# Two transformer blocks on one core: the SBUF pools in another order, and two buffer sizes changed, so that float32r operands start at multiples of 128 bytes

## Chip, cores and metric

One core of one Trainium2 chip. The metric is the device time of one execution in microseconds (us); lower is better.

## The reference, cut to what matters

Two blocks work on one sequence of 256 tokens with 2048 features, in float32. Block 1 mixes by attention (8 heads of 128) and by a gated linear recurrence, then runs 32 experts of which each token uses two, then a gated per-layer input. Block 2 has 16 self-attention heads of three kinds, an attention to 256 memory rows and a convolutional gated feed-forward of width 5632, and a last norm. Nearly all of the arithmetic is in the dense products with the weights:

```python
proj = hn @ w_in[i]                                       # 2048 x 5128, and a second one in block 2
h = h + jnp.concatenate([att_out, rnn_out], axis=-1) @ w_out[i]
hid = jax.nn.silu(t @ w_gate[e]) * (t @ w_up[e])          # experts
gate = jax.nn.sigmoid(rms_norm(h, ple_norm[i]) @ w_ple_gate[i])
# block 2, feed-forward: 2048 -> 2 x 5632 -> 2048
```

## The kernel before

**Products of high accuracy from float32r.** Every dense product is made three times. A weight arrives as float32 in a `raw` buffer. ScalarE copies 1024 columns of it, rounded to float32r, into a `hi` buffer (`split_hi`), and VectorE writes what the rounding lost into a `lo` buffer (`split_lo`). The tokens are kept in the same way as a pair of operands (`xth` and `xtl`, `xtuh` and `xtul`, and so on), in the big slots S0 to S5. A product is hi*hi + lo*hi + hi*lo, all in float32r, accumulated in PSUM; `mm` (line 506) issues each of these TensorE products.

There are two forms. In `form_a` a block of 128 weight columns is stationary, and all 256 tokens move: one product has 256 columns. In `form_b` the tokens, 128 at a time, are stationary and the weights move: one product has 512 columns. For each product the stationary operand is loaded anew (LDWEIGHTS, "PEld" in the profile).

**Order of the work.** The weights come as a list of units (`units`), at most 128 x 2048 float32, each loaded by the SyncE queue into one of 5 `raw` buffers. A unit is cut into quarters of 1024 columns. Each quarter takes the next of 4 `hi` and 4 `lo` buffers in turn, so quarter after quarter goes round the four buffers. In the up projection of the last feed-forward a quarter makes 2 x 4 x 3 = 24 products of 256 columns, in the down projection 2 x 2 x 3 = 12 products of 512 columns. All other work beside the products is written as tasks; a model of the engines' clocks (`clk`) decides at build time in which order instructions are emitted. Its costs are computed from the shapes of the operands that an instruction reads and writes, and not from the sizes or the addresses of the buffers that hold them. The experts (lines 1263 to 1565) work in float32 on the weights as they are loaded, and use the slots, the `raw` buffers and the `hi` and `lo` buffers as targets of their loads; the gathering and adding up of tokens around them is in float32r.

**Where the buffers lie.** A pool takes its place in each partition of SBUF in the order in which the pools are opened (lines 35 to 41), and within a pool the buffers lie one behind the other, each rounded up to 32 bytes. The pools begin at byte 16,512 of a partition, which is 129 x 128. First comes `per` with 25,632 bytes of constants and small tiles. So `slots`, 6 buffers of 16,384 bytes, begins at 42,144; that is 32 bytes past a multiple of 64, and 160 past a multiple of 256, and so does each slot in it. `stm` follows with 5 `raw` buffers of 4 x 520 x 4 = 8,320 bytes, then 4 `hi` and 4 `lo` buffers of 1040 x 4 = 4,160 bytes; 4,160 is 65 x 64. So the four `hi` buffers start at 32, 96, 160 and 224 bytes past a multiple of 256, and the four `lo` buffers likewise, in the same order. `wk`, 6 buffers of 2,048 bytes, and `sm` come last.

The operand slices add multiples of 512 bytes (`form_a`: 128 columns; `form_b`: 128 tokens of a row of 1024 bytes) or 1024 bytes to these starts, so a product's operands stand past a multiple of 256 as their buffers do. The one exception is the first product of block 1, whose units are 520 columns wide: there the blocks of 128 columns begin 8 columns (32 bytes) into a row, and the second row of a unit stands another 2,080 bytes on, so that some stationary operands start at multiples of 64 while the moving ones stay at 160 past a multiple of 256.

Of the kernel before, what the change touches and what calls it, by code (L numbers as in the profile page):

```python
# [30 lines left out]
def block_kernel(ctx: ExitStack, tc: tile.TileContext, A, out, stop=None, dbg=None, force_general=False):  # L31
# [3 lines left out]
    per = ctx.enter_context(tc.tile_pool(name="per", bufs=1))  # L35
    slots = ctx.enter_context(tc.tile_pool(name="slots", bufs=1))
    stm = ctx.enter_context(tc.tile_pool(name="stm", bufs=3))
    wk = ctx.enter_context(tc.tile_pool(name="wk", bufs=1))
    sm = ctx.enter_context(tc.tile_pool(name="sm", bufs=8))
# [7 lines left out]
    # ------------------------------------------------------------------ order of emission  # L47
    # Every engine takes its instructions in the order in which they are emitted. Work beside the matrix products
    # is cut into tasks: generators that name the engine ("a", "d", "p") before each of their steps. A model of
    # the engines' clocks (us) picks the step that can start first, so that no engine waits for another one  # L50
    # inside a chain while it has other work.
# [18 lines left out]
    class Vec:  # L70
        def __getattr__(self, name):
            f = getattr(nc.vector, name)

            def g(o, *a, **k):
                f(o, *a, **k)  # L75
                ins = [x for x in a[:3] if not isinstance(x, (float, int)) and x is not None]
                fast = name in ("tensor_scalar", "tensor_copy", "memset") and all(x.space != PSM for x in ins)
                t = 0.068 + o.free_size() * (0.00052 if fast else 0.00104)
                if name == "tensor_reduce":
                    t = 0.068 + ins[0].free_size() * 0.00104  # L80
                if name in ("tensor_scalar", "scalar_tensor_tensor") and not isinstance(a[1], (float, int)):
                    t += 0.06
                now = clk["d"]
                # an operand that the last instruction has just written costs its latency
                w = last.get("o")
                if o.free_size() <= 64 and any(x.tensor is w for x in ins):
                    t += 0.13
                last["o"] = o.tensor
                clk["d"] = now + t
            return g  # L90
# [4 lines left out]
    def mul(o, l, r, start, stop):  # L95
        """a product beside the stream"""
        nc.tensor.matmul(o, l, r, start=start, stop=stop, skip_group_check=True)  # L97
        clk["p"] += r.free_size() * (1 if r.dtype == F32R or r.dtype == BF else 4) / 2400.0 + 0.01
# [64 lines left out]
    def advance(t):  # L163
        """run the task to its next request; False when it has ended"""
# [17 lines left out]
    def settle(t):  # L182
        """resolve conditions and delays; True when the task asks for an engine"""
# [39 lines left out]
    def candidates(qs):  # L223
        """[(start, priority, run it, engine)]"""
# [16 lines left out]
    def pump():  # L241
        """what fits beside the products that have been emitted"""
# [32 lines left out]
    # ------------------------------------------------------------------ weight stream  # L275
# [86 lines left out]
    def raw_tile():  # L362
        return stm.tile([128, 4 * 520], F32, name="raw", tag="raw", bufs=RAWS)

    def hl_tiles(dtype):
        return (stm.tile([128, 1040], dtype, name="hi", tag="hi", bufs=HLS),
                stm.tile([128, 1040], dtype, name="lo", tag="lo", bufs=HLS))

    # buffers of the experts' weights: two slots in halves, the raw tiles, the tiles of the split weights, and
    # at first a third slot  # L370
# [13 lines left out]
    def exp_bufs(x):  # L384
# [3 lines left out]
        if k == "R":  # L388
            t = raw_tile()[:, 0:2048]
# [31 lines left out]
    # the third slot is free after the raw tiles and most of the split weights' that come behind it  # L421
# [12 lines left out]
    def split_steps_open():  # L434
        """the steps of splitting that could be next: [(start, quarter, run it)]"""
# [35 lines left out]
    def next_quarter():  # L471
# [11 lines left out]
        if EXP0 - RAWS <= u < EXP0:  # L483
            # the first of the experts' weights, as tiles get free
# [12 lines left out]
    def need_of(done):  # L497
        """products wait until the blocks up to kb are there"""
# [9 lines left out]
    def form_a(X, kbs, blocks, first, last, need=None, beside=True):  # L508
        """W stationary: blocks = [(psum out [128, S], column, first in its bank)]"""
# [21 lines left out]
    def form_b(X, kbs, banks, first, last, width=512, need=None):  # L531
        """X stationary: banks[tt] psum [128, <=512]"""
# [37 lines left out]
    # ------------------------------------------------------------------ start: loads and constants  # L570
# [13 lines left out]
    # x and the first weights in turns; when they are there, about  # L584
# [16 lines left out]
    def warm(n):  # L601
        """products that nobody reads: the tensor engine's clock rises only after some us of work"""
# [16 lines left out]
    # the other constants, as rows to be transposed  # L619
# [30 lines left out]
    def const_gen():  # L650
# [19 lines left out]
        # half biases of the gates; 2 softplus(-lam), by atanh's series for log1p  # L670
# [37 lines left out]
    # ------------------------------------------------------------------ norms: sums over d, 1/rms per token  # L708
    def rsqrt(n, ssq, scale):
        """[128, n] 1/sqrt(ssq * scale + EPS)"""  # L710
# [18 lines left out]
    def have_r():  # L729
        """the condition that the norm asked for last is there"""  # L730
# [3 lines left out]
    def spread(r):  # L734
        """[128 tok, 2] per-token factors -> [128, 256] on all partitions, in PSUM"""
# [5 lines left out]
    def set_r(ssq, wide):  # L741
        """a task's steps: R["r"] [128 tok, 2] and R["b"] [128, 256] from sums of squares [128 tok, 2]"""
# [32 lines left out]
    def add_sq(sq, t):  # L775
        """the sum of the blocks' squares, by one more"""
# [6 lines left out]
    def operand(dst, kb, gain, sq, t, done):  # L783
        """a task's steps: block kb of h times the gain as an operand, and its squares"""
# [10 lines left out]
    def resid_gen(o, kb, dst, gain, sq, done):  # L795
        """h += o; operand of the next norm"""
# [4 lines left out]
    def split_steps(dst, kb, src, done=None):  # L801
        """a task's steps: an operand of src"""
# [19 lines left out]
    # ================================================================== block 1: mixing  # L822
# [49 lines left out]
    def bias_rows_gen():  # L872
        """relative-position bias of block 2, to DRAM:
        bias_d[head, q, c] = row[head, 127 - q + c], queries 128..255 at keys 0..255"""
# [31 lines left out]
    # minus the sums of log f, in three parts that add up to it exactly, at partitions 0, 32 and 64  # L906
# [61 lines left out]
    def rnn_gen():  # L968
        """scan; rc becomes the state.
        a = exp(-y), s = tanh(y/2): 1/(1+s) = (1+a)/2, refined; a = 2/(1+s) - 1; sqrt(1-a^2) = 2 sqrt(s)/(1+s)"""  # L970
# [27 lines left out]
    # F and RX  # L998
# [17 lines left out]
    # Q, K: per-head norms, transposed  # L1016
# [48 lines left out]
    # attention of block 1  # L1065
    def max_of(srcs, biases, p, m):
        """scores + bias -> p [128, 384], -max in m[2:4]"""
# [13 lines left out]
    def pt_steps(p):  # L1081
        """P [128 q, 384] -> P^T: [128 s0, 256 t] | [128 s1, 128 t]"""
# [11 lines left out]
    def pv_t(t, v, dst, kb, done=None):  # L1094
        """out^T [dh, tok] = V^T P^T, split into dst"""
# [46 lines left out]
    # RG: gelu(rg) * state  # L1142
# [27 lines left out]
    # w_out; tokens in rows for the experts; scores of the router  # L1170
# [33 lines left out]
    def xn_gen(n, tt):  # L1204
# [9 lines left out]
        if n == 3:  # L1214
            # beside the routing on the vector engine
# [46 lines left out]
    # ================================================================== block 1: experts  # L1262
# [22 lines left out]
    # groups of a token: [128, (tt), 4]; experts: [128, (tt, group), 8]. The choice does not depend on the token's  # L1285
    # 1/rms, a positive factor of all its scores; the first of equal ones is taken
# [31 lines left out]
    # place among the expert's tokens from 1 on where selected, 0 elsewhere  # L1318
# [17 lines left out]
    def gather(q):  # L1336
        """the tokens of four experts' slots: xe, by steps of two of its 16 rows"""
# [22 lines left out]
    def weights():  # L1360
        """weights of the two experts, times 1/rms of the token; what goes past the slots"""
# [39 lines left out]
    def loadable(u):  # L1401
        """whether the unit's buffer has been read"""
# [14 lines left out]
    def hidden(i):  # L1417
        """the experts' hidden values of pair i, times the slots' weights, and room for their transpose"""
# [42 lines left out]
    def transposes(i):  # L1461
        """of the hidden values, and of G"""
# [29 lines left out]
    # the first pair's hidden values beside its gather  # L1492
# [13 lines left out]
    for i in range(16):  # L1506
# [7 lines left out]
        if i == 15:  # L1514
            # p^T as an operand
# [9 lines left out]
        for j in range(2):  # L1525
# [16 lines left out]
            if i == 15:  # L1542
                # the next weights are split in time for the products that follow
# [27 lines left out]
    # general path: the tokens past an expert's slots, by dense products over all tokens  # L1571
# [54 lines left out]
    # ================================================================== block 1: gated per-layer input  # L1626
# [52 lines left out]
    # ================================================================== block 2: self attention  # L1679
# [134 lines left out]
    # w_out_2; the memory's operands beside it  # L1814
# [81 lines left out]
    # ================================================================== block 2: memory attention  # L1896
# [98 lines left out]
    # ================================================================== block 2: conv-GLU  # L1995
# [25 lines left out]
    def tok_gen():  # L2021
        """h in place to tokens in rows: h[p, kb, (tt, c)]"""
# [64 lines left out]
    # w_down: hid split as it is used; tokens in rows  # L2087
# [22 lines left out]
    def fin_gen(bank, n, tt):  # L2110
        """h += products (tokens in rows), sums of squares; times the final gain, but for the last columns"""
# [37 lines left out]
    def last_columns(X, banks):  # L2149
        """the last products of the last two column blocks, one token tile after the other"""  # L2150
# [40 lines left out]
def _constants():  # L2191
    """rows of a product with [bias table; ones; dilated heads]: distance d = 255 - i of column i"""
# [42 lines left out]
```

## Time and profile before

| | |
|---|---|
| time, median of 3 runs | 2263.07 us (2262.58 to 2263.34) |
| span of the profiled execution, first to last instruction | 2260.5 us |
| the median less that span | 2.6 us |
| TensorE products in the trace | 15,552 |
| weights and inputs read from HBM | 510.61 MB |

PE is the matrix products, PEld the loads of stationary operands, DVE VectorE, ACT ScalarE. The products are pipelined: a row of the trace gives a product's whole passage through the array, and the next product starts well before it ends. What a product costs in a stream is therefore the distance from its start to the next start, called the pitch here. It is read from two starts and the number of products between them, or from a piece of the chain that has only such products.

### The profile page before, as it was taken

How to read it: one execution, taken by the hardware profiler on the slowest of the kernel's cores; microseconds unless marked ns; L12 is line 12 of the kernel's file. 1: busy time of each engine (PE TensorE's matmuls, PEld its weight loads, DVE VectorE, ACT ScalarE, POOL GpSimd, SP SyncE). 2: the span in 40 equal slices, each digit the busy share in tenths (PEclk: the TensorE clock that was granted, in tenths of full speed). 3: DMA queues.
4: the chain of work that ended last, by engine and by line, in shares of the span. 5: the costliest groups of instructions: out<-in, count | busy, mean ns of one | idle time of the engine just before them, and what ended most of it. 6: DMA issues, size and time to landing. Idle time of an engine off the chain costs nothing.

```text
span 2260.5 us, 37736 instructions
## 1 busy us (share of the span) xinstructions
PE 2210.5 (98%) x15552; PEld 1887.0 (83%) x15552; DVE 1264.3 (56%) x2251; ACT 943.7 (42%) x1493; POOL 34.0 (2%) x62
## 2 busy tenths in 40 slices
PE   9999979999999999999999999999999999999998
PEld 8888978555455565998999999999999999988886
DVE  8866654233333334875477558675655665564545
ACT  6745533211111112654444446455444444444443
POOL 1000000000000000000000000000000000000000
PEclk9999989999999999999999999999999999999999
DMA  8554668999999997465545556555555565555552
GB/s 282 168 180 164 144 189 304 332 403 396 401 398 396 399 394 276 171 196 194 185 153 170 181 180 192 184 169 170 187 187 188 185 195 191 191 200 193 186 187 93
DMA packets 232415, 517.30 MB, mean 229 GB/s; under 512 B 11783, under 2 KB 51446, under 8 KB 232112
## 3 DMA queue, kind: packets, MB, share of 16 engines
q1 hardware_dynamic: 229168, 506.57, 63.7%
q0 software_dynamic: 3040, 8.27, 1.8%
q8 instruction: 124, 2.03, 0.4%
q14 instruction: 51, 0.42, 0.1%
q10 hardware_dynamic: 32, 0.01, 0.0%
HBM read 510.61 MB, written 4.19 MB: 228 GB/s over the span
## 4 chain that ended last, share of the span: by engine, by line
PE 59%; DVE 0%; ACT 0%; ACTq 0%; issue 0%
PE acc L506 51%; PE sd L506 6%; PE sd L97 2%; PE sd L699 1%; DVE rs L75 0%; DVE hid L75 0%; DVE lo L75 0%; ACT hi L61 0%; ACT junk L61 0%; ACT out L61 0%; DVE h L75 0%; ACT cx L61 0%; DVE hs L75 0%; ACTq L2231 0%; ACT xtph L61 0%
## 5 line engine op out<-in xcount | busy, mean ns | idle before, releaser
L75 DVE TENSOR_TENSOR lo<-raw,hi 128x1024 fp32r<-128x1024 f32 (+1 forms) x572 | 698.6, 1224 | 549.2 <-ACT hi L61 544.1
L61 ACT ACTIVATE hi<-raw 128x1024 fp32r<-128x1024 f32 (+1 forms) x572 | 605.6, 1059 | 768.8 <-PE acc L506 649.2
L506 PE MATMUL acc<-xtuh,hi 128*128 128x256 f32 x1408 | 393.9, 280 | 0.0
L506 PE MATMUL acc<-xtul,hi 128*128 128x256 f32 x1408 | 393.6, 280 | 0.0
L506 PE MATMUL acc<-xtuh,lo 128*128 128x256 f32 x1408 | 393.2, 279 | 0.0
L506 PEld LDWEIGHTS acc<-xtuh,lo 128*128 128x128 f32 x1408 | 266.1, 189 | 0.0
L506 PEld LDWEIGHTS acc<-xtuh,hi 128*128 128x128 f32 x1408 | 266.0, 189 | 0.0
L506 PEld LDWEIGHTS acc<-xtul,hi 128*128 128x128 f32 x1408 | 265.8, 189 | 0.0
L75 DVE TENSOR_TENSOR h<-acc,h 128x512 f32<-128x512 f32 (+1 forms) x180 | 101.7, 613 | 196.0 <-PE acc L506 196.0
L506 PE MATMUL acc<-xt2h,hi 128*128 128x256 f32 x512 | 147.5, 288 | 0.0
L506 PE MATMUL acc<-xt2l,hi 128*128 128x256 f32 x512 | 143.4, 280 | 0.0
L506 PE MATMUL acc<-xt2h,lo 128*128 128x256 f32 x512 | 143.4, 280 | 0.0
L506 PE MATMUL acc<-hi,hs 128*128 128x512 f32 x352 | 112.0, 393 | 0.8 <-ACT hs L61 0.7
L506 PE MATMUL sd<-hi,hs 128*128 128x512 f32 x352 | 111.7, 393 | 0.0
L61 ACT ACTIVATE sg<-acc,ws 128x256 f32<-128x256 f32 x16 | 7.6, 475 | 243.6 <-PE acc L1445 148.2
L506 PEld LDWEIGHTS acc<-xt2h,hi 128*128 128x128 f32 x512 | 96.8, 189 | 4.1 <-issue 4.0
L506 PEld LDWEIGHTS acc<-xt2l,hi 128*128 128x128 f32 x512 | 96.9, 189 | 0.1
L506 PEld LDWEIGHTS acc<-xt2h,lo 128*128 128x128 f32 x512 | 96.7, 189 | 0.0
L75 DVE TENSOR_TENSOR yy<-acc,yy 128x512 fp32r<-128x512 f32 x64 | 44.3, 692 | 92.4 <-ACT yy L61 92.4
L506 PEld LDWEIGHTS acc<-gt,yy 128*128 128x128 f32 x512 | 64.4, 188 | 30.4 <-issue 27.7
L506 PE MATMUL acc<-oth,lo 128*128 128x256 f32 x256 | 72.8, 284 | 12.3 <-DVE lo L75 12.3
L506 PEld LDWEIGHTS acc<-hi,hs 128*128 128x128 f32 x352 | 66.0, 188 | 16.4 <-ACT hs L61 0.9
(390 smaller groups left out, 4711.3 us busy)
## 6 DMA issues: line engine op xcount, KB each, us to landing
raw<-in_w_up_dram SPq DMA_DIRECT2D x88, 1024.0 KB, 5.0
raw<-in_w_in_dram SPq DMA_DIRECT2D x52, 1024.0 KB, 5.2
raw<-in_w_down_dram SPq DMA_DIRECT2D x44, 1024.0 KB, 5.0
raw<-in_w_out_dram SPq DMA_DIRECT2D x32, 1024.0 KB, 5.1
raw<-in_w_in_dram SPq DMA_DIRECT2D x64, 512.0 KB, 4.5
raw<-in_w_expert_down_dram SPq DMA_DIRECT2D x29, 1024.0 KB, 10.1
raw<-in_w_expert_gate_dram SPq DMA_DIRECT2D x45, 512.0 KB, 10.0
raw<-in_w_expert_up_dram SPq DMA_DIRECT2D x45, 512.0 KB, 10.2
```

What stands on the lines that cost most here:

```text
L61: nc.scalar.activation(o, i, f, **k)
L75: f(o, *a, **k)
L97: nc.tensor.matmul(o, l, r, start=start, stop=stop, skip_group_check=True)
L506: nc.tensor.matmul(o, l, r, start=first, stop=last, skip_group_check=True)
L699: nc.tensor.transpose(o, i, idt)
```

## The change

The pool `per` is opened after `wk` and no longer first. The `raw` buffers become 2,048 elements (8,192 bytes) in place of 2,080, and the `hi` and `lo` buffers 1,056 elements (4,224 bytes, 33 x 128) in place of 1,040. The rest of the diff takes out comments and docstrings. No instruction is added, taken out or given another shape.

```diff
-    per = ctx.enter_context(tc.tile_pool(name="per", bufs=1))
     slots = ctx.enter_context(tc.tile_pool(name="slots", bufs=1))
     stm = ctx.enter_context(tc.tile_pool(name="stm", bufs=3))
     wk = ctx.enter_context(tc.tile_pool(name="wk", bufs=1))
+    per = ctx.enter_context(tc.tile_pool(name="per", bufs=1))
     sm = ctx.enter_context(tc.tile_pool(name="sm", bufs=8))
...
     def raw_tile():
-        return stm.tile([128, 4 * 520], F32, name="raw", tag="raw", bufs=RAWS)
+        return stm.tile([128, 2048], F32, name="raw", tag="raw", bufs=RAWS)
 
     def hl_tiles(dtype):
-        return (stm.tile([128, 1040], dtype, name="hi", tag="hi", bufs=HLS),
-                stm.tile([128, 1040], dtype, name="lo", tag="lo", bufs=HLS))
+        return (stm.tile([128, 1056], dtype, name="hi", tag="hi", bufs=HLS),
+                stm.tile([128, 1056], dtype, name="lo", tag="lo", bufs=HLS))
...
         if k == "R":
-            t = raw_tile()[:, 0:2048]
+            t = raw_tile()
```

By the same count as above `slots` now begins at 16,512, the `raw` buffers at 114,816, the `hi` buffers at 155,776, the `lo` buffers at 172,672 and `wk` at 189,568: all multiples of 128. Past a multiple of 256 the slots stand at 128, and the four `hi` and the four `lo` buffers at 128, 0, 128 and 0.

## Rows read from the trace of the kernel before

**Rows 1.** The page, its first part: span, and busy time by engine.

```profile
span 2260.5 us, 37736 instructions
PE 2210.5 (98%) x15552; PEld 1887.0 (83%) x15552; DVE 1264.3 (56%) x2251; ACT 943.7 (42%) x1493; POOL 34.0 (2%) x62
```

**Rows 2.** Busy time in stretches, line 506 alone: PE, PEld, granted clock, DMA share, GB/s.

```profile
11.00:200.00 189.00, 173.95 (x940) 146.72 (x939) 1.00 0.59 197
200.00:460.00 260.00, 157.03 (x1226) 150.40 (x1224) 0.96 0.74 239
...
905.00:1127.00 222.00, 219.34 (x1560) 205.51 (x1560) 0.99 0.57 188
1127.00:1326.00 199.00, 174.54 (x1392) 166.66 (x1392) 1.00 0.52 168
1326.00:1420.00 94.00, 91.01 (x767) 89.98 (x768) 1.00 0.56 180
1420.00:1558.00 138.00, 127.73 (x966) 120.24 (x966) 1.00 0.53 177
1558.00:2006.00 448.00, 447.28 (x3841) 447.08 (x3839) 1.00 0.58 188
2006.00:2260.50 254.50, 244.41 (x1056) 198.02 (x1056) 0.98 0.50 170
```

**Rows 3.** The same view, all instructions: PE, PEld, DVE, ACT, POOL busy, clock, DMA, GB/s.

```profile
0.00:57.00 57.00, 54.57 (x421) 50.49 (x421) 46.26 (x115) 35.27 (x62) 8.63 (x21) 1.00 0.82 280
452.00:509.00 57.00, 55.21 (x373) 32.94 (x370) 19.84 (x37) 9.87 (x21) 0.00 (x0) 1.00 1.03 403
...
791.00:848.00 57.00, 55.22 (x390) 34.42 (x388) 17.77 (x34) 8.23 (x19) 0.00 (x0) 1.00 1.02 394
```

**Rows 4.** The chain that ended last: start us, length us, what.

```profile
1557.90 444.46 PE acc L506 x3815
...
2023.15 11.09 PE acc L506 x48
```

**Rows 5.** Timeline of PE in the up projection, first products of five quarters in a row.

```profile
1700.45 0.28 PE L506 MATMUL acc<-xtuh,hi 128*128 128x256 f32 x1
...
1703.17 0.28 PE L506 MATMUL acc<-xtuh,hi 128*128 128x256 f32 x1
...
1706.01 0.28 PE L506 MATMUL acc<-xtuh,hi 128*128 128x256 f32 x1
...
1708.75 0.28 PE L506 MATMUL acc<-xtuh,hi 128*128 128x256 f32 x1
...
1711.63 0.28 PE L506 MATMUL acc<-xtuh,hi 128*128 128x256 f32 x1
```

**Rows 6.** The same view in the down projection: products of 512 columns.

```profile
2080.03 0.39 PE L506 MATMUL sd<-lo,hs 128*128 128x512 f32 x1
...
2080.71 0.39 PE L506 MATMUL sd<-lo,hs 128*128 128x512 f32 x1
...
2081.40 0.39 PE L506 MATMUL sd<-lo,hs 128*128 128x512 f32 x1
...
2082.10 0.39 PE L506 MATMUL sd<-lo,hs 128*128 128x512 f32 x1
```

**Rows 7.** The same view: plain float32 transposes, and float32 products in two passes.

```profile
55.33 1.89 PE L97 MATMUL sd<-vrc,qkT 128*128 128x256 f32 x8
...
1462.30 1.47 PE L699 MATMUL sd<-ident,pm 128*128 128x128 f32 x12
```

**Rows 8.** Lines, shapes kept apart: the splitting of the weights on DVE and ACT.

```profile
L75 DVE TENSOR_TENSOR lo<-raw,hi 128x1024 fp32r<-128x1024 f32 x564 | 688.7, 1224 | 546.3 <-ACT hi L61 541.2 <-PE sd L97 2.6 <-DMA eraw<-in_w_expert_up_dram 1.6
L61 ACT ACTIVATE hi<-raw 128x1024 fp32r<-128x1024 f32 x564 | 596.9, 1059 | 762.4 <-PE acc L506 648.4 <-PE sd L506 75.4 <-issue 24.8
```

**Rows 9.** The first product (units 520 columns wide), stationary at other offsets.

```profile
26.23 0.28 PE L506 MATMUL acc<-xth,hi 128*128 128x256 f32 x1
...
27.55 0.28 PE L506 MATMUL acc<-xth,lo 128*128 128x256 f32 x1
```

**Rows 10.** DMA issues on the page: KB each, us to landing.

```profile
raw<-in_w_up_dram SPq DMA_DIRECT2D x88, 1024.0 KB, 5.0
```

## Prediction

> **What bounds the kernel now.** I read the page's first part for who is busy, then the stretches for where, then the chain and the timeline for what one product costs. TensorE is busy for 2210.5 of 2260.5 us, VectorE for 56% and ScalarE for 42% [rows 1]. A busy PE alone does not say that PE is the bound, so the stages are read one by one. The line that issues the float32r products is busy for nearly the whole of every stretch after 905 us [rows 2]. One stage has another limit: in the experts, 460 to 905 us, the DMA engines are saturated up to about 850 us (share 1.02 and more, 394 to 403 GB/s) [rows 3], and a faster product there only waits longer for its weights. Between 200 and 460 us line 506 is busy for 157.03 of 260 us, with waits in between [rows 2].
>
> In the chain, 3815 products of 256 columns take 444.46 us with nothing between them, 116.5 ns each; 48 products of 512 columns take 11.09 us, 231 ns each [rows 4]. The granted clock is 1.00 in these stretches (2.4 GHz). One column a cycle would be 106.7 and 213.3 ns, so the stream loses 8% of both. The loss has a pattern. Quarter after quarter, with the same instructions and the same moving operands, the pitch changes: 2.72 us for 24 products is 113.3 ns, then 2.84 gives 118.3, 2.74 gives 114.2, 2.88 gives 120.0, and the cycle begins again [rows 5]. What differs is the weights' buffer, which stands at 96, 32, 224 and 160 past a multiple of 256. So addresses matter here, and in steps: 113.3 is 17 times 6.67 ns and 120.0 is 18 times, where 6.67 ns is 16 columns, 64 bytes of one partition. With 512 columns, three products take 0.68 us in one quarter and 0.70 in the next [rows 6]: 226.7 and 233.3 ns, 34 and 35 such steps. An operand of 1024 bytes that starts 32 past a multiple of 64 touches 17 pieces of 64 bytes; one that starts on a multiple touches 16. That is my reading. One thing is against it: 2048 bytes touch 33 pieces and not 34, so a long operand seems to pay twice.
>
> Two more rows bound what is left when the cost is gone. Twelve float32 transposes, each with its own load of 128 stationary columns, come at (1.47 - 0.27) / 11 = 109 ns; float32 products of 256 columns, at half speed, come at (1.89 - 0.38) / 7 = 216 ns a pass, 2.7 ns above two cycles a column, although their operands stand at 32 past a multiple of 64 too [rows 7]. At half speed a bad start costs nothing that can be seen.
>
> **The change, part by part.** No instruction goes, comes or moves, on any engine or queue; the planner's costs come from shapes, so the order of emission is the same. What changes is every operand's address.
>
> *Products of 256 columns.* All stood at 32 past a multiple of 64 (moving and stationary); all will stand on multiples of 128. The best that I can take from a row is 109 ns, since each product must still load 128 stationary columns and the transposes show that at 109 [rows 7]. From 116.5 this is 7.5 ns, 6.4%. Bounds: 106.7 below (8.4%), and above 119.2, the mean of the two worse offsets, for the reason in the second rival (2.3% slower).
>
> *Products of 512 columns.* From 231 to 216, two cycles' worth of a float32 pass with its 2.7 ns [rows 7]: 15 ns, 6.5%. Bounds: 213.3 (7.7%) and no change.
>
> *Where it counts.* Line 506 is busy for 1635.3 us outside 460 to 905 us. Of the 157.03 us between 200 and 460 us I count half, since PE waits for attention and for operands there: 1556.8 us. Times 6.45% this is 100.4 us. In the experts I count nothing: the DMA hides it. The span becomes 2160.1 us; the median stood 2.6 us above the span, so the time is **2163 us**.
>
> *Loads into buffers at other addresses.* In the experts the rate stays between 394 and 403 GB/s [rows 3] while loads go to all four kinds of offset. I take nothing, with 1% of 390 us, 4 us, either way in the bounds.
>
> *ScalarE and VectorE.* Splitting costs 1059 and 1224 ns a quarter [rows 8]. Nothing shows a dependence on addresses; bounds a few per cent either way, hidden since a quarter lasts 2.8 us. What is late next: in the first 57 us VectorE is busy for 46.26 us [rows 3]; 6.45% less PE time would raise that from 81% to 87%, still under the cover.
>
> *The smaller* `raw` *buffers* hold the same 2048 elements; the cost is nothing. They do come free sooner when PE is faster: 48 products of the up projection ask for 1 MB in 5.2 us in place of 5.6, and a load lands in 5.0 us [rows 10], with several in flight. This cover holds, though the margin per load is thin.
>
> **The rivals.**
>
> *Part of the gain (chance 0.22).* A step is saved where the moving operand starts well, but loads of the stationary operand still collide with it. Then all quarters run as the best ones do now: 113.3 for 256 columns (2.7% of 1312.4 us, 35.4 us) and 226.7 for 512 columns (1.9% of 244.4 us, 4.6 us), which gives 2223 us; the case reaches from 2190 to 2258. For it: the same moving operand runs at 113.3 or 120.0 by the stationary one's offset alone, so some collision exists. A stationary operand on a multiple of 64, with the moving one still off it, gives (27.55 - 26.23) / 11 = 120 ns [rows 9]: aligning the stationary one alone buys nothing. Against it: the excess of a 512-column product is twice that of a 256-column one, though it loads the same stationary columns; the moving operand carries most of the cost.
>
> *Relative place decides; slower (chance 0.14).* The moving operand stands at 160 past a multiple of 256. The slow quarters are those whose stationary operand stands 0 or 128 away from it, 120.0 and 118.3; the fast ones are 64 or 192 away. After the change the slots stand at 128 and the `hi` and `lo` buffers at 128 and 0: every pair is 0 or 128 apart, and the good distances are gone. If only the distance counts, every quarter of 256 columns runs at 119.2 ns, 2.3% more over 1312.4 us, 30 us: 2293 us. It decides if the pitch of the up projection comes out above 116.5 ns in all four buffers. Against it: it leaves the loss of the 512-column products unexplained. A sentence apart: the Trainium skill, "TensorE: Matmul & The Clock Gate", section "Step-by-step: what each phase is for", says that moving and stationary operands have independent read ports, so that a load takes nothing from a running product. By that rule this rival would fall; the trace disagrees at 113.3 against 120.0 ns.
>
> *No effect (chance 0.09).* The pitch may depend on the place among 256 bytes in a way that multiples of 128 do not improve on the mean: fast and slow buffers mix as now, and the time stays at 2263 us, within 4.5. For it: no product in the trace has a moving float32r operand on a multiple of 64, so the gain is nowhere shown. Against it: four pitches for four offsets. A sentence apart: the Trainium skill, "SBUF — State Buffer", section "Door 1: The DMA port swizzle", puts the lines of SBUF at 16 bytes, and every operand here starts on such a line before and after. By that rule nothing would change; four pitches at starts that are all multiples of 32 speak against it.
>
> **How the numbers follow.** The full effect, 2123 to 2190 us, has 0.55; part of it 0.22; no effect 0.09; slower 0.14. The forecast is that of the first. The range begins at 2123: 8.3% of 1635.3 us is 136 us, and 4 us for the loads. It ends at 2252, inside the partial case, and so leaves out no effect, slower and little else. Faster by over 0.2% (4.5 us, about what a measurement of this kernel tells from no change) has 0.55 + 0.22 = 0.77, within 0.2% 0.09, slower 0.14.
>
> **What would show it.** Right: in the changed trace the up projection's 24 products last about 2.62 us in every quarter and no longer change from buffer to buffer; 48 products of the down projection take about 10.4 us in the chain; the experts' stretch keeps its length; counts of instructions are the same. Partial: quarters of 2.72 us. Wrong: quarters of 2.8 us or more, or a pitch that still goes round with the four buffers.

## The result, and the profile after

The changed kernel takes **2283.18 us** (2282.30 to 2283.60 in 4 runs) where the kernel before takes 2262.97 us in 4 runs: a ratio of 1.0091 [1.0077, 1.0106]. It is **slower by 20 us**, outside the range and on the other side of the forecast, in the direction of the second rival. That is under 1%, but far outside the spread of either kernel's runs.

The page of the changed kernel; its line numbers are one higher than before, so line 506 is now 507:

```profile
span 2281.2 us, 37736 instructions
...
PE 2232.4 (98%) x15552; PEld 1910.9 (84%) x15552; DVE 1266.1 (56%) x2251; ACT 944.1 (41%) x1493; POOL 34.0 (1%) x62
...
L76 DVE TENSOR_TENSOR lo<-raw,hi 128x1024 fp32r<-128x1024 f32 (+1 forms) x572 | 698.4, 1223 | 563.7 <-ACT hi L62 560.2
L62 ACT ACTIVATE hi<-raw 128x1024 fp32r<-128x1024 f32 (+1 forms) x572 | 605.7, 1059 | 788.6 <-PE acc L507 675.0
...
raw<-in_w_up_dram SPq DMA_DIRECT2D x88, 1024.0 KB, 4.9
```

Beside [rows 1, 8, 10]: every engine has the same number of instructions, a split still costs 1059 ns on ScalarE and 1223 on VectorE, and a load lands in 4.9 us in place of 5.0. TensorE alone has changed by more than 2 us: PE is busy for 21.9 us more and PEld for 23.9, and the span is 20.7 us longer. It is not the clock: the mean granted clock is 0.992 before and 0.993 after.

Line 507 by its operands, with the duration of one product in ns (shortest, median, longest) and the start of the first and of the last in us; the duration of one is not the pitch at which they follow one another:

```profile
L507 PE MATMUL acc<-xtuh,hi x1408: 277/283/367, 1518.6 to 2026.2; 128*128 128x256 f32 x176
...
L507 PE MATMUL acc<-hi,hs x352: 389/392/498, 2027.4 to 2270.8; 128*128 128x512 f32 x176
L507 PE MATMUL acc<-xth,hi x272: 274/282/471, 7.6 to 267.9; 128*128 128x256 f32 x136
L507 PE MATMUL acc<-oth,hi x256: 274/283/420, 268.2 to 381.2; 128*128 128x256 f32 x128
...
L507 PE MATMUL acc<-xtph,hi x256: 277/283/581, 908.3 to 1008.9; 128*128 128x256 f32 x128
...
L507 PE MATMUL acc<-ot2h,hi x256: 278/283/469, 1318.8 to 1417.4; 128*128 128x256 f32 x128
```

In the kernel before, the same view has the first products of these stages at 8.1 (`xth`), 268.5 (`oth`), 905.6 (`xtph`), 1311.4 (`ot2h`), 1508.1 (`xtuh`) and 2005.9 us (`hs`). Taking the stages from first product to first product: nothing is lost up to 268 us, 3.0 us from there to 905.6, 4.7 to 1311.4, 3.1 to 1508.1 (`ot2h` and what follows it), **11.0** in the up projection (497.8 to 508.8 us), and from 2005.9 us to the end 0.8 is won (254.6 to 253.8 us). That is the 20.7 us within rounding.

The chain of waits, up and down projection (start, length, what):

```profile
1569.13 457.61 PE acc L507 x3840
...
2044.57 11.05 PE acc L507 x48
```

457.61 / 3840 is 119.2 ns a product of 256 columns, where it was 116.5 [rows 4]; a product of 512 columns takes 230.2, where it was 231. PE still waits for nothing here. The products themselves have become slower, and the timeline shows which:

```profile
1703.40 0.28 PE L507 MATMUL acc<-xtuh,hi 128*128 128x256 f32 x1
...
1706.24 0.28 PE L507 MATMUL acc<-xtuh,hi 128*128 128x256 f32 x1
...
1709.12 0.28 PE L507 MATMUL acc<-xtuh,hi 128*128 128x256 f32 x1
...
1711.96 0.28 PE L507 MATMUL acc<-xtuh,hi 128*128 128x256 f32 x1
...
1714.84 0.28 PE L507 MATMUL acc<-xtuh,hi 128*128 128x256 f32 x1
```

The quarters of 24 products last 2.84, 2.88, 2.84 and 2.88 us: 118.3 and 120.0 ns in turn. Quarters of 2.8 us or more were what the prediction named as the sign of being wrong. The fast quarters of [rows 5], 2.72 and 2.74 us, are gone. The weights' buffers stand at 0 and 128 past a multiple of 256 and the moving operand at 128, so the two are 128 or 0 apart, and the two pitches are those that the kernel before showed at these distances.

In the experts nothing has changed, as the stretch from 460 to 850 us shows (PE, PEld, DVE, ACT, POOL busy, granted clock, DMA share, GB/s); the kernel before moved 399 GB/s in it, at the same share:

```profile
460.00:850.00 390.00, 378.85 (x2376) 212.41 (x2374) 127.33 (x235) 63.55 (x135) 0.00 (x0) 1.00 1.02 398
```

### The profile page after: what moved, and what is told of

The parts are those of the page before. It is cut to its first block, busy times and chain, and to the rows that moved or that the text cites. A ratio compares the mean times of both kernels' runs of the same rounds, so it can differ in the third digit from the quotient of the medians.

```text
span 2281.2 us, 37736 instructions
## 1 busy us (share of the span) xinstructions
PE 2232.4 (98%) x15552; PEld 1910.9 (84%) x15552; DVE 1266.1 (56%) x2251; ACT 944.1 (41%) x1493; POOL 34.0 (1%) x62
## 4 chain that ended last, share of the span: by engine, by line
PE 60%; ACT 0%; DVE 0%; ACTq 0%; issue 0%
PE acc L507 52%; PE sd L507 6%; PE sd L98 2%; PE sd L700 1%; DVE rs L76 0%; ACT junk L62 0%; ACT out L62 0%; DVE h L76 0%; ACT cx L62 0%; ACT hs L62 0%; ACTq L2232 0%; ACT xtph L62 0%; DVE s L76 0%; ACTq L62 0%
## 5 line engine op out<-in xcount | busy, mean ns | idle before, releaser
L76 DVE TENSOR_TENSOR lo<-raw,hi 128x1024 fp32r<-128x1024 f32 (+1 forms) x572 | 698.4, 1223 | 563.7 <-ACT hi L62 560.2
L62 ACT ACTIVATE hi<-raw 128x1024 fp32r<-128x1024 f32 (+1 forms) x572 | 605.7, 1059 | 788.6 <-PE acc L507 675.0
L507 PEld LDWEIGHTS acc<-xt2h,hi 128*128 128x128 f32 x512 | 97.3, 190 | 4.1 <-issue 4.0
L507 PEld LDWEIGHTS acc<-xt2l,hi 128*128 128x128 f32 x512 | 97.3, 190 | 0.1
```

What stands on the lines that cost most here:

```text
L62: nc.scalar.activation(o, i, f, **k)
L507: nc.tensor.matmul(o, l, r, start=first, stop=last, skip_group_check=True)
```

## The experiments

Throughout, the **distance** of a pair is the start of the weights' buffer less the start of the other operand, past a multiple of 256 bytes. In the products of 256 columns the weights are the stationary operand; in the down projection, of 512 columns, they are the moving one. The distances follow from the sizes of the buffers; where a buffer starts is counted from the first byte of the pools, and no trace shows an address. Two theories stand against each other: *distance* (the pitch hangs on how the two operands stand to each other) and *alignment* (it hangs on where each of them starts).

**64 empty bytes ahead of the weights' buffers.** The changed kernel, with all operands on multiples of 64, but `hi` and `lo` 64 bytes further on, so that the distances are 64 and 192:

```diff
     slots = ctx.enter_context(tc.tile_pool(name="slots", bufs=1))
+    gap = ctx.enter_context(tc.tile_pool(name="gap", bufs=1))
+    gap.tile([128, 16], F32, name="gap")
     stm = ctx.enter_context(tc.tile_pool(name="stm", bufs=3))
```

> The changed kernel with 64 empty bytes between the slots and the weights' buffers: slots stay on multiples of 128, raw, hi and lo stand 64 past them. Distance theory (what counts is where the stationary operand stands against the moving one, modulo 256): all quarters are 64 or 192 apart, so the up projection runs at about 114 ns a product in every quarter (before showed 113.3 and 114.2 there); 119.2 less 114 times some 9,700 products is 50 us less than the changed kernel, the 512-column products stay near 231: about 2236 us. Alignment theory (multiples of 128 are what helps, and something else in the new layout cost more): nothing is won when hi and lo leave the multiples of 128, 2283 us or more.

Measured: 2235.95 us, ratio to before 0.9882 [0.9866, 0.9899]. Run again on another chip, beside the kernels further down, it gave 2236.46 us, 0.9890 [0.9874, 0.9907]. The chain of the first run (line 507 is 509 here):

```profile
1545.32 432.40 PE acc L509 x3815
```

and its timeline of PE, the first products of three quarters in a row:

```profile
1694.78 0.28 PE L509 MATMUL acc<-xtuh,hi 128*128 128x256 f32 x1
...
1697.50 0.28 PE L509 MATMUL acc<-xtuh,hi 128*128 128x256 f32 x1
...
1700.22 0.28 PE L509 MATMUL acc<-xtuh,hi 128*128 128x256 f32 x1
```

432.40 / 3815 is 113.3 ns, and the quarters shown last 2.72 us each. Outside the up projection and the experts, products of 256 columns came to 114.9 ns on average (steps from start to start under 135 ns, which leaves waits out), so not every stage reached 113.3. 64 bytes that nothing reads are worth 47.2 us to the changed kernel (2283.18 to 2235.95).

**The same distances without alignment.** The kernel before, every operand 32 past a multiple of 64 as it was, with the same gap and the larger `hi` and `lo`:

```diff
+    gap = ctx.enter_context(tc.tile_pool(name="gap", bufs=1))
+    gap.tile([128, 16], F32, name="gap")
     stm = ctx.enter_context(tc.tile_pool(name="stm", bufs=3))
...
-        return (stm.tile([128, 1040], dtype, name="hi", tag="hi", bufs=HLS),
-                stm.tile([128, 1040], dtype, name="lo", tag="lo", bufs=HLS))
+        return (stm.tile([128, 1056], dtype, name="hi", tag="hi", bufs=HLS),
+                stm.tile([128, 1056], dtype, name="lo", tag="lo", bufs=HLS))
```

> The kernel before, per still first and raw still 2,080 elements, with hi and lo of 1,056 elements and 64 empty bytes ahead of stm: every float32r operand stands 32 past a multiple of 64 as before, and all quarters are 64 or 192 apart. Distance theory: the same pitch of about 114 ns as with aligned operands, about 2236 us, within 5 us of e1_gap64. Alignment theory: no better than before, 2263 us, and slower than e1_gap64 by 20 us or more.

Measured: 2236.25 us, 0.9886 [0.9869, 0.9902]. The chain:

```profile
1543.98 432.50 PE acc L508 x3815
```

113.4 ns a product. With good distances it makes 0.3 us whether the operands start on multiples of 64 or 32 past one, which is less than the runs of one kernel differ. Alignment by itself buys nothing; this alone ends the forecast's theory.

**Which part of the change costs.** The changed kernel with `hi` and `lo` at their old size, so that the pool order and the smaller `raw` remain and the four buffers stand again at four distances:

```diff
-        return (stm.tile([128, 1056], dtype, name="hi", tag="hi", bufs=HLS),
-                stm.tile([128, 1056], dtype, name="lo", tag="lo", bufs=HLS))
+        return (stm.tile([128, 1040], dtype, name="hi", tag="hi", bufs=HLS),
+                stm.tile([128, 1040], dtype, name="lo", tag="lo", bufs=HLS))
```

> The changed kernel with hi and lo of 1,040 elements as before: slots on multiples of 128, the four hi and lo buffers 0, 64, 128 and 192 away, the same four distances as in the kernel before, with all starts on multiples of 64. Distance theory: the time of the kernel before, 2263 us within 4, and pitches that go round from 113.4 to 120.0. Alignment theory: if multiples of 64 help, 2200 us or less; if the order of the pools is what cost, about 2283 us.

Measured: 2262.22 us, 1.0001 [0.9991, 1.0011], on 10 runs beside 13 of the kernel before. The chain:

```profile
1558.36 447.21 PE acc L507 x3840
```

447.21 / 3840 is 116.5 ns, the mean of before. So the order of the pools and the size of `raw` are worth nothing, although they alone put the operands on multiples of 64 (those of the 520-column units apart). The whole loss comes from the 64 bytes by which each `hi` and `lo` buffer grew: 4,160 bytes lead round four distances, 4,224 bytes only back and forth between two.

**The pitch by itself.** A program of nothing but such products: a moving and a stationary buffer, both beginning on multiples of 256, 48 products for each pair of starts, and all other engines idle. With 256 columns the stationary operand walks past the moving one, with 512 the moving one past the stationary, as the weights do in the kernel.

```diff
+    for i, d in enumerate(range(0, 256, 32)):
+        group("sta" + "abcdefgh"[i], 256, 0, d)      # columns, start of moving, start of stationary
...
+    for i, d in enumerate((4, 8, 16, 48, 80, 256, 320, 512, 576, 1088)):
+        group("fin" + "abcdefghij"[i], 256, 0, d)
...
+    for i, (m, d) in enumerate(((32, 0), (32, 64), (32, 128), (32, 192), (16, 0), (16, 64))):
+        group("shf" + "abcdef"[i], 256, m, m + d)
...
+    for i, d in enumerate(range(0, 256, 32)):
+        group("wid" + "abcdefgh"[i], 512, d, 0)
...
+    for i, (c, d) in enumerate(((256, 0), (256, 64), (512, 0), (512, 64))):
+        group("bfl" + "abcd"[i], c, 0, d, BF)
```

> Only products, 48 of one kind in a row, over the first 128 rows of x; none of the reference is computed. The stationary operand walks past the moving one in steps of 32 bytes, in finer steps and beyond 256 bytes; both are shifted together by 32 and 16 bytes; 512 columns; other widths; bfloat16. Distance theory: 256 columns run at about 120 ns at distance 0, 118 at 128, 114 at 64, 113.4 at 192, the same when both are shifted by 32 or 16 bytes, and distance 256 is like 0. Alignment theory: products with both on a multiple of 128 run at 109, all others at 113 or more. A third: without ScalarE, VectorE and DMA beside them all distances run at 109, since the collisions are with these engines.

The timeline of PE (start and length of a group of 48; a letter's distance is its place in the lists of the diff):

```profile
24.79 5.91 PE L46 MATMUL staa<-mov,sta 128*128 128x256 f32 x48
...
36.22 5.82 PE L46 MATMUL stac<-mov,sta 128*128 128x256 f32 x48
...
47.51 5.85 PE L46 MATMUL stae<-mov,sta 128*128 128x256 f32 x48
...
98.50 5.92 PE L46 MATMUL finf<-mov,sta 128*128 128x256 f32 x48
...
126.97 5.91 PE L46 MATMUL shfa<-mov,sta 128*128 128x256 f32 x48
132.72 5.82 PE L46 MATMUL shfb<-mov,sta 128*128 128x256 f32 x48
...
155.40 5.62 PE L46 MATMUL shff<-mov,sta 128*128 128x256 f32 x48
160.86 11.09 PE L46 MATMUL wida<-mov,sta 128*128 128x512 f32 x48
...
183.00 11.16 PE L46 MATMUL widc<-mov,sta 128*128 128x512 f32 x48
...
205.21 11.36 PE L46 MATMUL wide<-mov,sta 128*128 128x512 f32 x48
...
277.58 5.42 PE L46 MATMUL bfla<-mvb,stb 128*128 128x256 bf16 x48
282.83 5.40 PE L46 MATMUL bflb<-mvb,stb 128*128 128x256 bf16 x48
288.07 10.52 PE L46 MATMUL bflc<-mvb,stb 128*128 128x512 bf16 x47
298.43 10.52 PE L46 MATMUL bfld<-mvb,stb 128*128 128x512 bf16 x47
```

The pitch is the length less one product's own (0.28, or 0.39 us at 512 columns), over 47. Both operands on multiples of 256, distance 0: (5.91 - 0.28) / 47 = 119.8 ns, not 109. Distance 64 gives 117.9, 128 gives 118.5, 256 again what 0 gives (`finf`). Shifting both operands by 32 bytes leaves the same pitches (`shfa`, `shfb`). So the distance counts with every other engine idle, and for these starts it counts modulo 256. At 512 columns it is 227.7 at distance 0, 229.1 at 64 and 233.4 at 128. In bfloat16 neither distance matters: from start to start 109.4 and 109.2 ns, and (298.43 - 288.07) / 48 = 215.8 for 512 columns.

One thing missed: at the distances 64 and 192 the expectation was 113.4 to 114 ns, the kernel's pitch, and this bench gave 117.9 and 117.7, except in `shff` (both operands 16 bytes on, distance 64), with (5.62 - 0.28) / 47 = 113.6. So distance 64 has two pitches, and something else picks one of them. Nor is the distance everything for starts that the kernels do not have: with both operands 16 bytes on, distance 0 gave 118.3 in place of 119.8, and a stationary operand 8 bytes past the moving one gave 115.5.

**The kernel's order of operands.** The same bench with `hi` and `lo` and the sequence of products as in the kernel, at 16 distances; then, behind one product of another width, one pair repeated.

```diff
+    for i, d in enumerate(range(0, 256, 16)):
+        run("ker" + letters[i], like_kernel(d))
...
+    for i, (c, d) in enumerate([(c, d) for d in (64, 192) for c in (96, 160, 224, 300, 400)]):
+        run("led" + letters[i], [(0, 0, 0, d)], c)
+        run("aft" + letters[i], [(0, 0, 0, d)] * 48)
```

> Only products, over the first 128 rows of x; none of the reference is computed. First the kernel's order of operands (hi with the first moving tile, hi with the second, lo with the first, four column blocks) at distances from 0 to 240 bytes in steps of 16; then one operand pair repeated at 64 and 192 behind one product of another width; then pairs that are 64 apart for their own products but 0 or 128 from the product before, and the reverse; then 512 columns. If the pitch is set by the load of the next stationary operand against the moving operand that streams meanwhile: own-good pairs run at 118 or more and before-good pairs at 113 to 118 without being slower than pairs good in both ways. If it is set within one product, the reverse. If the 117.8 ns at 64 and 192 in the first map is a second state of the same distance, the lead-in products bring some groups to 113.3, and the kernel's order gives 113.3 to 114.1 at 64 and 192. If only odd multiples of 64 are good, no other step is under 117.

The timeline of PE: the first products of the groups at the distances 0, 16, 64, 80, 192 and 208, and then two of the groups behind a lead-in at distance 64 (of 160 and of 400 columns):

```profile
27.40 0.28 PE L43 MATMUL kera<-mvh,sth 128*128 128x256 f32 x1
...
33.15 0.28 PE L43 MATMUL kerb<-mvh,sth 128*128 128x256 f32 x1
...
50.17 0.28 PE L43 MATMUL kere<-mvh,sth 128*128 128x256 f32 x1
...
55.61 0.28 PE L43 MATMUL kerf<-mvh,sth 128*128 128x256 f32 x1
...
95.65 0.28 PE L43 MATMUL kerm<-mvh,sth 128*128 128x256 f32 x1
...
101.09 0.28 PE L43 MATMUL kern<-mvh,sth 128*128 128x256 f32 x1
...
123.88 5.85 PE L43 MATMUL aftb<-mvh,sth 128*128 128x256 f32 x48
...
141.31 5.61 PE L43 MATMUL afte<-mvh,sth 128*128 128x256 f32 x48
```

(55.61 - 50.17) / 48 and (101.09 - 95.65) / 48 are 113.3 ns, the kernel's pitch, at distances 64 and 192. Distance 0 has (33.15 - 27.40) / 48 = 119.8, and no other of the sixteen came under 116.6. Behind a lead-in of 400 columns a repeated pair at distance 64 runs at (5.61 - 0.28) / 47 = 113.4, and at 113.3 from its third product on. Behind one of 160 columns the same sum gives 118.5; its first step alone takes 154 ns, and from the third product on it stays at 117.8. Lead-ins of 96, 224 and 300 columns gave 117.8 as well. So at distance 64 the stream can settle in either of **two states**, by what ran just ahead of it, and in these groups it kept the one it had after a few products. At distance 192 no single pair left the worse one; only the kernel's order reached 113.3 there.

The same run had four groups in which two pairs alternate, to ask whether the moving operand that counts is the product's own or that of the product before. At 64 from its own but 0 and 128 from the one before the pitch was 118.6 ns; at 0 from its own but 192 and 64 from the one before, 117.1; at 64 from both, 117.8; at 0 from both, 120.0. That leans to the product before. The products of 512 columns in the kernel's order repeated the map: 227.9 ns at distance 0, 229.3 at 64, 233 to 234 at the other multiples of 32.

**All at one distance.** `hi` and `lo` of exactly 4,096 bytes, first with the gap (all eight at distance 64), then without (all at 0). The units 520 columns wide are split row by row, since two of their rows no longer fit.

```diff
-            un["nq"] = max(1, un["nkb"] * un["width"] // 1024)
+            un["nq"] = un["nkb"] if un["width"] > 512 else max(1, un["nkb"] * un["width"] // 1024)
...
-        return (stm.tile([128, 1056], dtype, name="hi", tag="hi", bufs=HLS),
-                stm.tile([128, 1056], dtype, name="lo", tag="lo", bufs=HLS))
+        return (stm.tile([128, 1024], dtype, name="hi", tag="hi", bufs=HLS),
+                stm.tile([128, 1024], dtype, name="lo", tag="lo", bufs=HLS))
```

> The kernel with 64 empty bytes, hi and lo cut to 1,024 elements (4,096 bytes), so that all eight stand 64 past the slots modulo 256; the 520-column units are split row by row (16 quarters for 8). Distance theory: 113.3 ns in every quarter of the up projection as with the 64-byte gap alone; in the down projection all quarters at 229.2 in place of 229.2 and 232.5, 1.6 ns on 2,016 products, 3 us: about 2233 us, 3 under the gap alone, with 2 us either way for the split first product.

> The 64-byte gap alone once more, beside the others on the same chip: 2236 us.

> The same as all_64 without the 64 empty bytes: everything on multiples of 128, all eight buffers at distance 0. Distance theory: 120.1 ns in every quarter of the up projection and 227.9 in the down projection; 6.5 ns on some 9,700 products is 63 us more than all_64, less 1.3 ns on 2,016: about 2293 us, the slowest of all. If distance 0 and 128 were a matter of the buffers' size and not of the distance, it would stay near 2240 us.

Measured on one chip: all at 64, 2236.58 us, 0.9886 [0.9870, 0.9903]; the gap alone once more, 2236.46 us (given above); all at 0, 2282.86 us, 1.0091 [1.0074, 1.0108]. The chain of the first:

```profile
1344.45 28.27 PE acc L509 x240
...
1546.55 432.41 PE acc L509 x3815
...
2043.54 10.99 PE acc L509 x48
```

its line view, in the stage of the second block's attention output:

```profile
L509 PE MATMUL acc<-ot2h,hi x256: 276/281/468, 1299.7 to 1397.0; 128*128 128x256 f32 x128
```

and the same stage in the kernel with the gap of 64 bytes and the larger buffers, in the first of its two runs, with the piece of its chain that belongs to the first piece above:

```profile
L509 PE MATMUL acc<-ot2h,hi x256: 276/276/468, 1302.5 to 1397.5; 128*128 128x256 f32 x128
```

```profile
1346.32 27.42 PE acc L509 x240
```

The chain of the second:

```profile
1570.32 460.81 PE acc L507 x3840
...
2048.73 10.88 PE acc L507 x48
```

All at 64, the down projection won the small gain that was looked for (10.99 us for 48, 229.0 ns, where the other gap kernel has 11.08), but the stage of `ot2h` took 97.3 us in place of 95.0. It is in the worse of the two states: 28.27 us for 240 products are 117.8 ns each, where the other gap kernel has 27.42 us, 114.3 ns. Both kernels have good distances only (64 alone here, 64 and 192 there); what picks the state in a kernel was not tried. The gain and the loss about cancel, and 3.6 us were missed.

All at 0, the up projection came out at 460.81 / 3840 = 120.0 ns as expected, but the level was missed by 10 us. The expectation took 6.5 ns a product between these two kernels for all of some 9,700 products of 256 columns. In the up projection that holds: from its first product to the first of the down projection it lasts 485.2 us all at 64 and 512.2 us all at 0. The 5,520 outside it and the experts went from 115.8 to 119.8 ns on average, 4.0 ns each, since with all distances good many of them were not at 113.3. And the 512-column products are at their best at distance 0 (10.88 / 48 = 226.7 ns, where the changed kernel has 230.2), which about pays for the 0.8 ns by which 256 columns are worse than in the changed kernel: both take 2283 us. Between all at 64 and all at 0, which differ in 64 empty bytes, lie 46.3 us.

**Which stream gives way.** A last bench let both operands walk on from product to product, so that a load collides either with the product before it or with its own:

```diff
+    for p, (step, lead) in zip("pqrstu", ((64, 400), (64, 96), (192, 400), (192, 96), (128, 400), (0, 400))):
...
+            run("own" + p + letters[i],
+                [(k % 2, 256 + k * step % 256, k % 2, 256 + (k * step + d) % 256) for k in range(48)])
```

> Only products, over the first 128 rows of x; none of the reference is computed. Both operands step on from product to product, by 64, 192, 128 or 0 bytes; each product's stationary operand is d = 0, 64, 128 or 192 from its own moving operand, and so d + step from the moving operand of the product before, which streams while it is loaded. Reading 1, the load collides with the product before: with a step of 64, d = 192 (distance 0 to the one before) is the steady 120.0, and d = 0 and 128 are 113.3 or 117.8; with a step of 192, d = 64 is the 120.0. Reading 2, it is the product's own distance: d = 0 is 120.0 at every step, and 64 and 192 are 113.3 or 117.8.

Neither reading came out. With both operands at rest, distance 64 settled at 113.3 ns after six products and 0 gave 120.0, as before. As soon as both walk, every group lies between 116.7 and 120.1 from its third product on, at all four distances and with either lead-in. At a step of 64 behind 400 columns, the first reading wanted 120.0 at d = 192 and the second at d = 0; these gave 117.7 and 118.5, and d = 64 gave 120.1. So the lean of the four groups above was not borne out, and which of the two reads waits for the other, if one does, stays open.

## Why the prediction was wrong

- **The step that failed** is "Products of 256 columns", with that of 512 beside it: 116.5 to 109 ns and 231 to 216, because the operands no longer straddle one more piece of 64 bytes. Operands on multiples of 256 run at 119.8 and 227.7 ns in the bench, and aligned and misaligned kernels with the same distances take 2235.95 and 2236.25 us. Nothing was lost by misalignment, so nothing could be won. The 33 pieces against 34, noted as "against it", were the sign that the count of pieces was the wrong reading of the 6.67 ns steps.
- **The floor was taken from rows of another kind.** The 109 ns of the transposes and the 216 of the float32 passes [rows 7] are reached by bfloat16 (109.2 to 109.4 and 215.8), but no stream of float32r products in any run came under 113.3 at 256 columns or 226.7 at 512. That these rows were free of the loss was true; that float32r products could be was never shown.
- **The second rival had the mechanism and its sign.** Its pitch for the up projection was 119.2 ns and 119.2 was measured; the two worse pitches alternate as it said, and its test (above 116.5 in all four buffers) is met. Its time was 10 us too long: it laid 2.3% on 1312.4 us of line 506. In the up projection that holds (11.0 us). Elsewhere it allowed 20 us and 10.8 were measured, and the traces show why. Some 215 of the 1312.4 us are products of 512 columns at 231 ns, which lost nothing: over all 2,016 of that width the pitch went from 231.1 to 230.3 ns. And the 5,520 products of 256 columns outside the up projection and the experts (steps under 135 ns) did come to 119.1 ns, as it said, but from 117.0 and not from 116.5, so that they lost 1.8%. These parts, 11.0 us, 11.7 us and 1.5 us the other way, add up to 21.2 us, where the span grew by 20.7.
- **Its "against" did not weigh.** That 512 columns lose more was put against it, but they hang on the distance too, only with other good places: 0 and 64 in place of 64 and 192. And the Trainium skill, "TensorE: Matmul & The Clock Gate", section "Step-by-step: what each phase is for", has a load of stationary columns take nothing from the read of the running product. For bfloat16 the bench agrees (109.4 and 109.2 ns at two distances); for float32r the pitch hangs on how the two operands stand to each other (119.8 at one distance, 117.9 or 113.4 at another), which two reads that take nothing from each other do not explain, and the measurement decides. The rows that carried this rival, 113.3 against 120.0 with one moving operand [rows 5], were shown evidence; those that carried the forecast were an inference to addresses that no row had. A chance of 0.14 was too low for that.
- **The partial case falls with the first.** It took the best quarters as what aligned operands reach. Every quarter can run at 113.3, and the gap kernels show it, but by distance, and the time is then 2236 us and not 2223: the 512-column products keep their pitch (4.6 us), the 2.7% were laid on some 215 us of such products in the other stages too (5.8 us), and those stages came to 114.9 ns and not to 113.3.
- **Right:** the same instructions on every engine, splits at the same 1059 and 1223 ns, the experts at 398 GB/s in place of 399 whatever the loads' targets, and no cost of the smaller `raw` or of the order of the pools (1.0001 [0.9991, 1.0011]).

## What to carry to other kernels

When a stream of float32r products has a pitch that goes round with the buffers, look at how the two operands stand to each other modulo 256 bytes, not at whether each is aligned: here 64 empty bytes turn the change from 0.9% slower than the kernel before into 1.2% faster (2235.95 us, the best version found). Rounding buffers up to a neat size can do harm, because it makes all of them fall on the same few distances. And where the rows show one thing varying, forecast from the values that occur in them; an address that no row has is a guess, however tidy the count behind it.

## What the runs showed of the hardware that was not expected

- Float32r products, each with its own load of 128 stationary columns, at a granted clock of 1.00: at 256 columns 113.3 ns (117.8 in the worse state) at the distances 64 and 192, 118.3 at 128, 120.0 at 0; at 512 columns, with the weights moving, 226.7 to 227.9 at 0, 229 at 64 and 233 at 128 and 192. The best distance for 512 columns, 0, is among the worst for 256. In the bench 384 columns too ran better at 0 than at 64 (174.0 and 176.7 ns), and 128 columns ran at 111.7 at either.
- The two states at one distance: 113.3 or 117.8 ns from the third to the 48th product of a row, by the width of the single product ahead of them (400 or 160 columns). In the kernels with good distances alone, 432.40 us of the up projection stay in the better one without a break, and other stages do not (117.8 ns in `ot2h` with all buffers at 64).
- Bfloat16 products of the same shapes ran alike at the two distances tried, 0 and 64 (109.2 to 109.4 and 215.8 ns); at 256 columns 3.5% under the best float32r pitch.
